# Row sums of squares in one accumulator, context operand made earlier, modulation rounds in pairs of steps ahead of the attention

## The chip, the cores and the metric

The kernel runs on one core of one Trainium2 chip. The metric is the device time in microseconds of one execution, by the median of several runs; less is better. In the profile PE is TensorE (PEld its weight loads), DVE is VectorE, ACT is ScalarE, POOL is GpSimd and SP is SyncE, which here only issues DMAs. PE reads its operands from SBUF and writes to PSUM, which has eight banks; the matmuls here run in fp32 or in a form of it (fp32r).

## What is computed

Two transformer blocks in a row on x, 512 positions by 1024 channels. What the change touches lies in the front of the first block:

```python
mod_l = jnp.split((jax.nn.silu(c) @ ada_w[l] + ada_b[l])[:, None, :], 6, axis=-1)
mod_c = jnp.split((jax.nn.silu(c_ctx) @ ada_w[l] + ada_b[l])[None, None, :], 6, axis=-1)

h = _modulate(_rmsnorm(x, norm1_g[l]), mod_l[0], mod_l[1])
hc = _modulate(_rmsnorm(xc, norm1_g[l]), mod_c[0], mod_c[1])
z = h @ w_in[l]
...
kvc = hc @ w_in[l][:, ATT_W:3 * ATT_W]
...
att = _neighbourhood_attention(q, k, v, kc, vc, na_rpb[l], rows)
y = _mix_out(att, z, ...)
x = x + mod_l[2] * y

h2 = _modulate(_rmsnorm(x, norm2_g[l]), mod_l[3], mod_l[4])
x = x + mod_l[5] * _conv_ffn(h2, ...)
```

`_rmsnorm` divides each row by the root of its mean square, and `_modulate(h, shift, scale)` is `h * (1 + scale) + shift`. Parts 0 and 1 of the modulation are needed at once, for h and hc; parts 2 to 5 only behind the attention. The second block (stick-breaking attention, a gated convolution, a feed-forward part) is not touched.

## The kernel before

Everything is kept transposed, channels on the 128 partitions, so that x is eight slices of 128 x 512 (`xs`) and the context eight of 128 x 256 (`cs`). A matmul in full precision is three matmuls (`mm3`, lines 164 to 166): each operand is split into a rounded high half and a rest (hi on ACT, lo on DVE).

The order on every engine is that of the code; each engine works through its own instructions in turn, and a wait holds all that stand behind it. SP issues its DMAs in program order too.

The front runs in these stages.

- **Row sums of squares of x.** For each slice as it lands, ACT or DVE (in turn) squares it, and PE adds it up over channels with four matmuls by a column of ones into `ssb` (line 485), 32 matmuls in all. `rsqrt_col` makes the reciprocal root of it (ACT's root, then DVE), `bcast` spreads that over the partitions by four matmuls, and ACT copies it into `rxs`.
- **First projection** (`first_*`). For each of eight slices k: 1 MB of modulation weights arrives (`first_ada`), `first_rows` multiplies it by the conditioning columns (16 records on PE), `first_mod` turns the result into shift and scale of slice k, `first_h` makes h[k], `first_split` splits 128 x 768 of the weights w_in, and `first_mm` adds 18 matmuls into six banks `first`.
- **u and q** (`p_u`, `p_q`): four weight pieces of 256 columns. Beside them the taps of a depthwise convolution of length 31 run on DVE (`tap_v`), some after every tile.
- **Context operand** (`make_hc`): for each slice k of the context, DVE multiplies, ACT adds the shift and rounds (hi), DVE makes the rest (lo). Two slices are made per call: slices 0 and 1 behind the first tile of the last query piece, 2 and 3 behind its second, 4 and 5 behind the first value tile, 6 and 7 behind the second.
- **v** (`v_tile`): four tiles from h, then two from hc (the first uses of hc), for each half of the columns; keys (`keys`, from h and hc) partly between the two halves, partly inside the attention.
- **Attention**: a loop over 32 blocks n. In one pass PE makes the scores of block n (`s`), turns the weights of block n-3 (`pt`) and applies those of n-6 (`o`); DVE adds the bias and finds the minimum (`e`, line 889), ACT takes the exponent, DVE its reciprocal (`rd`), POOL scales. `e` of block n stands on DVE behind `rd` of block n-1, which waits for ACT's exponent of n-1.
- **Rest of the modulation** (`ada_*`). Parts 2 to 5 are two rounds of eight steps. `ada_fetch` issues the four DMAs of a step (1 MB), `ada_step` runs its four matmuls (128 x 512, eight records) into a bank, `ada_end` finishes a round. `ada_tick` ends a round if one is due, fetches one step, and runs one step if more than two are fetched. It is called behind most tiles of u, q and v, and in the attention from block 7 on (AD0) at every second block. So seven steps run ahead of the first context value tile, the eighth behind the second one, the first round ends in the second half of v, and the second round's eight steps and its end lie in the attention.

Tiles lie in a pool of 80 slots of 128 x 512, reused when their readers are done; weight pieces in three buffers `wraw`, so that a DMA into one waits until DVE has split what was there.

Of the kernel before, what the change touches and what calls it, by code (L numbers as in the profile page):

```python
# [9 lines left out]
F32 = mybir.dt.float32  # L10
# [111 lines left out]
AD0 = 7  # L122
# [13 lines left out]
def program(ctx: ExitStack, tc: tile.TileContext, A, outT):  # L136
# [14 lines left out]
    def bank(name="bank", cols=T):  # L151
        return ps.tile([P, cols], F32, tag="b", name=name, padded_shape=[P, T])
# [324 lines left out]
    ssb = bank("sums", cols=4)  # L477
    for k in range(KD):
        t = slot(name="sq")
        if k % 2:  # L480
            V.tensor_mul(t, xs[k], xs[k])
        else:
            S.activation(t, xs[k], AF.Square)
        for i in range(4):
            PE.matmul(ssb[:, i : i + 1], t[:, i * P : (i + 1) * P], ones, start=k == 0 and i == 0,
                      stop=k == KD - 1, skip_group_check=True)
# [8 lines left out]
    def first_w(p):  # L495
        wr = wraw_p.tile([P, 2048], F32, tag="wraw", name="wraw")[:, : 2 * NF * P].rearrange("p (k n) -> p k n", k=2)
        nc.sync.dma_start(wr, w_in[p * 256 : (p + 1) * 256, W0 : W0 + NF * P].rearrange("(k p) n -> p k n", p=P))
        for kk in range(2):
            fw[2 * p + kk] = wr[:, kk, :]
# [44 lines left out]

    first_ada(0)
    first_w(0)
    first_ada(1)
    first_ada(2)
    first_w(1)
    first_rows(0)  # L550
    rx = rsqrt_col(ssb, 4)
    first_split(0)
    first_mod(0)
    rxb = bcast(rx, 4)
    rxs = slot(name="rxs")
    S.activation(rxs, rxb, AF.Copy)
    first_h(0)
    first_rows(1)
    first_split(1)
    first_mod(1)  # L560
    first_h(1)
    first += [bank(f"first{m}") for m in range(NF)]
    for k in range(KD):
        if k + 3 < KD:
            first_ada(k + 3)
        if k in (1, 3):
            first_w(2 + k // 2)
        if k == 5:
            ws.load(0)
        if k + 2 < KD:  # L570
            first_rows(k + 2)
            first_split(k + 2)
        first_mm(k, range(3))
        if k + 2 < KD:
            first_mod(k + 2)
            first_h(k + 2)
        first_mm(k, range(3, NF))
        del fw[k]
    ws.need(0)
# [59 lines left out]

    ROUNDS = (4, 5, 8, 9), (6, 7, 10, 11)  # L640
    ada_live, ada_todo, ada_bank = [], [(r, kk) for r in range(2) for kk in range(KD)], {}

    def ada_fetch():
        if ada_todo:
            r, kk = ada_todo.pop(0)
            raw = [slot(name="ada") for _ in range(4)]
            for t, c in zip(raw, ROUNDS[r]):
                nc.sync.dma_start(t, A["ada_w"][kk * P : (kk + 1) * P, c * T : (c + 1) * T])
            ada_live.append((r, kk, raw))

    def ada_step():
        r, kk, raw = ada_live.pop(0)
        if kk == 0:
            ada_bank[r] = bank("adab")
        for g in range(4):
            ada_matmul(ada_bank[r], g, kk, raw[g], kk == 0, kk == KD - 1)
        if kk == KD - 1:
            t = slot(name="arow")
            S.activation(t, ada_bank[r], AF.Copy)
            ada_ends.append((r, t))  # L660

    def ada_end():
        r, t = ada_ends.pop(0)
        b = ada_bank.pop(r)
        for q in range(4):
            PE.matmul(b[:, 4 * q : 4 * q + 4], t[:, q * P : (q + 1) * P], pick, start=True, stop=True)
        for g in (0, 2):
            j = 4 * ROUNDS[r][g]
            V.tensor_add(mod[:, j : j + 8].rearrange("p (g q) -> p g q", q=4),
                         b[:, :16].rearrange("p (q g) -> p g q", g=4)[:, g : g + 2],  # L670
                         pc("ada_b", j, 8).rearrange("p (g q) -> p g q", q=4))

    ada_ends = []

    def ada_tick(ahead=2):
        if ada_ends:
            ada_end()
        ada_fetch()
        if len(ada_live) > ahead or not ada_todo and ada_live:
            ada_step()  # L680

# [13 lines left out]
    ada_fetch()  # L695
    run(tiles(p_u, (0,), h, evac_u))
    ada_fetch()
# [32 lines left out]
    ada_tick()  # L730
    rcbs = slot(name="rcbs", cols=CTX)
    S.activation(rcbs, bcast(rc[0], 2), AF.Copy)
    hc = [None] * KD
# [19 lines left out]
    for i in range(4):  # L753
        V.tensor_scalar(vt_[i], vt_[i], mv[:, 2 * i : 2 * i + 1], sd[:, i : i + 1], op0=ALU.subtract, op1=ALU.mult)
        G.tensor_mul(vt_[i], vt_[i], rows[0][:, 0:256])
        G.tensor_add(vt_[i], vt_[i], rows[0][:, 256:512])
        t = slot(F32R, "vn")
        vn.append((t[:, :256], t[:, 256:]))
    for m in range(2):
        run(tiles(p_q[1], (m,), h, lambda m, b: evac_q(2 + m, b)))  # L760
        make_hc(2 * m, 2 * m + 1)
        ada_tick()
# [68 lines left out]
    for i in range(4):  # L831
        v_tile(p_v[0], 0, h, i, vt[i])
        if i < 2:
            make_hc(4 + 2 * i, 5 + 2 * i)
        split(*vn[i], vt_[i])
        if i % 2:
            ada_tick()
    for i in range(2):
        v_tile(p_v[0], 0, hc, i, vc[i])
    ada_step()  # L840
# [167 lines left out]
    for n in range(NA + OUT + 1):  # L1008
# [45 lines left out]
        if n >= AD0 and (n - AD0) % 2 == 0 and (ada_todo or ada_live or ada_ends):  # L1054
            ada_tick()
# [528 lines left out]
```

## Time and profile before

| | us |
|---|---|
| median of three runs | 1434.5 (1433.75 to 1435.11) |
| the profiled execution | 1432.46 |
| its span, first to last instruction | 1430.7 |
| mean granted clock of PE | 0.988 of full |

A row of the profile groups equal instructions or shows single ones: L485 is line 485 of the kernel, `out<-in` names the tiles, and what stands in brackets is how long the engine had sat idle and what ended that. Records of PE are pipelined and overlap, so a step of work is read from the start of one matmul to the start of the next. One fp32 matmul that isn't fp32r shows as two records.

### The profile page before, as it was taken

The numbers are of one execution on the slowest core, as the hardware profiler recorded it, in microseconds if no ns is written. First come the engines' busy times: TensorE is split into PE (matmuls) and PEld (weight loads), VectorE is DVE, ScalarE is ACT, GpSimd is POOL, SyncE is SP. The second block draws the span as 40 slices with busy tenths as digits, with TensorE's granted clock in tenths as the row PEclk, the third lists the DMA queues.
The fourth block names the chain that finished last, engine by engine and source line by source line (L and its number), as shares of the span: only waits on it lengthen the run. The fifth ranks groups of instructions, "written<-read, shape, count | busy, mean of one in ns | idle before, by whom it ended". The sixth has DMA issues, their size and how long they took to land.

```text
span 1430.7 us, 18856 instructions
## 1 busy us (share of the span) xinstructions
PE 1397.2 (98%) x7594; PEld 1175.1 (82%) x7594; DVE 776.9 (54%) x1138; ACT 555.5 (39%) x888; POOL 223.2 (16%) x210
## 2 busy tenths in 40 slices
PE   8997999999999999999999999999999999999996
PEld 6776986889888888888988888888888888888886
DVE  3578675746444344344448874445266866664224
ACT  3342255635433333233345543223454444443221
POOL 0021213110201111022010112000161111110102
PEclk9998999999999999999999999999999999999998
DMA  9574257332223222323164113222311322322221
GB/s 355 173 261 148 78 155 243 97 122 89 89 88 118 87 90 70 111 93 102 54 194 131 60 60 112 94 89 90 117 58 61 118 88 91 115 82 81 82 80 59
DMA packets 141878, 160.42 MB, mean 112 GB/s; under 512 B 5600, under 2 KB 119520, under 8 KB 141792
## 3 DMA queue, kind: packets, MB, share of 16 engines
q1 hardware_dynamic: 140352, 156.91, 33.8%
q10 hardware_dynamic: 1440, 2.31, 0.5%
q8 instruction: 59, 0.97, 0.3%
q14 instruction: 27, 0.22, 0.0%
HBM read 147.67 MB, written 2.10 MB: 105 GB/s over the span
## 4 chain that ended last, share of the span: by engine, by line
PE 75%; DVE 4%; ACT 1%; POOL 1%; issue 1%; DVEq 0%; POOLq 0%; ACTq 0%
PE bank L165 23%; PE bank L164 23%; PE bank L166 23%; PE z L1366 1%; PE sums L383 1%; POOL acc L1503 1%; DVE wlo L210 1%; PE v L164 1%; PE v L165 1%; PE v L166 1%; PE wT L1387 1%; PE bc L391 0%; DVE fo L1558 0%; DVE fo L1554 0%; PE o L164 0%
## 5 line engine op out<-in xcount | busy, mean ns | idle before, releaser
L210 DVE TENSOR_TENSOR wlo<-wraw,whi 128x1024 fp32r<-128x1024 f32 (+1 forms) x214 | 278.4, 1308 | 140.0 <-ACT whi L202 139.9
L165 PE MATMUL bank<-h_lo,whi 128*128 128x512 f32 (+1 forms) x816 | 306.2, 375 | 0.1
L166 PE MATMUL bank<-h_hi,wlo 128*128 128x512 f32 (+1 forms) x816 | 304.9, 374 | 0.8 <-DVE wlo L210 0.8
L164 PE MATMUL bank<-h_hi,whi 128*128 128x512 f32 (+1 forms) x816 | 305.7, 375 | 0.0
L202 ACT ACTIVATE whi<-wraw 128x1024 fp32r<-128x1024 f32 (+1 forms) x214 | 220.6, 1035 | 121.4 <-PE bank L165 107.3
L164 PEld LDWEIGHTS bank<-h_hi,whi 128*128 128x128 f32 x816 | 154.1, 189 | 28.6 <-ACT u L684 0.8
L166 PEld LDWEIGHTS bank<-h_hi,wlo 128*128 128x128 f32 x816 | 154.0, 189 | 28.7 <-DVE wlo L210 1.6
L165 PEld LDWEIGHTS bank<-h_lo,whi 128*128 128x128 f32 x816 | 154.1, 189 | 28.2 <-DVE h_lo L1494 0.3
L164 PE MATMUL bank<-act_hi,whi 128*128 128x512 f32 (+1 forms) x374 | 141.1, 377 | 0.8 <-ACT sq L1477 0.8
L165 PE MATMUL bank<-act_lo,whi 128*128 128x512 f32 (+1 forms) x374 | 140.8, 376 | 0.0
L166 PE MATMUL bank<-act_hi,wlo 128*128 128x512 f32 (+1 forms) x374 | 140.8, 376 | 0.0
L172 POOL TENSOR_TENSOR act_lo<-cv,act_hi 128x512 fp32r<-128x512 f32 x44 | 61.2, 1392 | 422.2 <-ACT act_hi L171 384.2
L164 PE MATMUL bank<-hb_hi,whi 128*128 128x512 f32 x288 | 115.8, 402 | 0.0
L166 PE MATMUL bank<-hb_hi,wlo 128*128 128x512 f32 x288 | 112.6, 391 | 0.0
L165 PE MATMUL bank<-hb_lo,whi 128*128 128x512 f32 x288 | 112.4, 390 | 0.0
L164 PEld LDWEIGHTS bank<-act_hi,whi 128*128 128x128 f32 x374 | 70.4, 188 | 14.0 <-ACT sq L1477 1.0
L166 PEld LDWEIGHTS bank<-act_hi,wlo 128*128 128x128 f32 x374 | 70.4, 188 | 13.0
L165 PEld LDWEIGHTS bank<-act_lo,whi 128*128 128x128 f32 x374 | 70.4, 188 | 12.8
L171 ACT ACTIVATE act_hi<-cv 128x512 fp32r<-128x512 f32 x44 | 27.8, 633 | 129.3 <-DVE cv L1208 72.9
L166 PEld LDWEIGHTS bank<-hb_hi,wlo 128*128 128x128 f32 x288 | 54.1, 188 | 11.5
L164 PEld LDWEIGHTS bank<-hb_hi,whi 128*128 128x128 f32 x288 | 54.2, 188 | 9.4
L165 PEld LDWEIGHTS bank<-hb_lo,whi 128*128 128x128 f32 x288 | 54.3, 188 | 9.1
(359 smaller groups left out, 2375.9 us busy)
## 6 DMA issues: line engine op xcount, KB each, us to landing
wraw<-in_w_in SPq DMA_DIRECT2D x23, 1024.0 KB, 5.1
wraw<-in_ffn_w_up SPq DMA_DIRECT2D x22, 1024.0 KB, 4.9
wraw<-in_w_up SPq DMA_DIRECT2D x22, 1024.0 KB, 4.9
ada<-in_ada_w SPq DMA_DIRECT2D x64, 256.0 KB, 5.7
ada<-in_ada_first SPq DMA_DIRECT2D x32, 256.0 KB, 6.5
wraw<-in_w_out SPq DMA_DIRECT2D x8, 1024.0 KB, 5.2
wraw<-in_ffn_w_down SPq DMA_DIRECT2D x8, 1024.0 KB, 5.0
wraw<-in_w_down SPq DMA_DIRECT2D x8, 1024.0 KB, 5.0
```

The costliest lines, as they stand in the source:

```text
L164: PE.matmul(out, lhs[0], rhs[0], start=start, stop=False, **kw)
L165: PE.matmul(out, lhs[0], rhs[1], start=False, stop=False, **kw)
L166: PE.matmul(out, lhs[1], rhs[0], start=False, stop=stop, **kw)
L171: S.activation(hi, src, AF.Copy)
L172: (eng or V).tensor_sub(lo, src, hi)
L202: S.activation(h, src, AF.Copy)
L210: V.tensor_sub(l, src, h)
L383: PE.matmul(b[:, i : i + 1], a[:, blk * P : (blk + 1) * P], ones, start=(j == 0), stop=(j == len(parts) - 1))
L1366: PE.matmul(z, qs2[hp][a][j][:, b * P : (b + 1) * P], ks2[hp][j][:, :nk], start=a == 0, stop=a == 1)
L1387: PE.transpose(pt[:, c * P : (c + 1) * P], w_[:, c * P : (c + 1) * P], ident)
L1503: G.tensor_add(acc3[:, ts], acc3[:, ts], t)
```

## The change

Four things change.

1. **Sums of squares.** ACT squares all eight slices; DVE adds the squares of slices 0 to 6 into one accumulator `xacc`; PE sums over channels once, by eight matmuls (`col_sums` of the accumulator and the last square). The root is taken ahead of the first `first_rows`, the copy `arow` stands behind it on ACT.
2. **First weights.** `first_w` loads 384 KB for one slice instead of 768 KB for two, each behind the modulation weights of its slice.
3. **Context operand.** `make_hc(0, 1)` stands ahead of the last query piece, and each later pair one tile earlier; 6 and 7 are made behind the first value tile.
4. **Modulation.** `ada_tick` runs two steps (and a fetch behind each) if so many are fetched; five steps are fetched inside the first projection (k from 3 to 7); there is a tick behind the first tile of u, and none in the attention. All sixteen steps run ahead of the first context value tile, in eight ticks of two. The first round ends behind the first tile of the last query piece, the second in the second half of v.

```diff
-    ssb = bank("sums", cols=4)
+    xacc = slot(name="xacc")
     for k in range(KD):
-        t = slot(name="sq")
-        if k % 2:
-            V.tensor_mul(t, xs[k], xs[k])
-        else:
-            S.activation(t, xs[k], AF.Square)
-        for i in range(4):
-            PE.matmul(ssb[:, i : i + 1], t[:, i * P : (i + 1) * P], ones, start=k == 0 and i == 0,
-                      stop=k == KD - 1, skip_group_check=True)
+        xsq = xacc if k == 0 else slot(name="sq")
+        S.activation(xsq, xs[k], AF.Square)
+        if 0 < k < KD - 1:
+            V.tensor_add(xacc, xacc, xsq)
     sqrt_table()
...
     def first_w(p):
-        wr = wraw_p.tile([P, 2048], F32, tag="wraw", name="wraw")[:, : 2 * NF * P].rearrange("p (k n) -> p k n", k=2)
-        nc.sync.dma_start(wr, w_in[p * 256 : (p + 1) * 256, W0 : W0 + NF * P].rearrange("(k p) n -> p k n", p=P))
-        for kk in range(2):
-            fw[2 * p + kk] = wr[:, kk, :]
+        if p % 2 == 0:
+            wr_[0] = wraw_p.tile([P, 2048], F32, tag="wraw", name="wraw")
+        fw[p] = wr_[0][:, p % 2 * 1024 : p % 2 * 1024 + NF * P]
+        nc.sync.dma_start(fw[p], w_in[p * P : (p + 1) * P, W0 : W0 + NF * P])
...
-    def ada_tick(ahead=2):
+    def ada_tick(n=2):
         if ada_ends:
             ada_end()
-        ada_fetch()
-        if len(ada_live) > ahead or not ada_todo and ada_live:
+        for _ in range(min(n, len(ada_live))):
             ada_step()
+            ada_fetch()
...
-    first_ada(0)
-    first_w(0)
-    first_ada(1)
-    first_ada(2)
-    first_w(1)
-    first_rows(0)
-    rx = rsqrt_col(ssb, 4)
+    for k in range(3):
+        first_ada(k)
+        first_w(k)
+    rx = rsqrt_col(col_sums((xacc, xsq), range(4)), 4)
     first_split(0)
-    first_mod(0)
+    first_rows(0)
     rxb = bcast(rx, 4)
+    first_mod(0)
...
     for k in range(KD):
         if k + 3 < KD:
             first_ada(k + 3)
-        if k in (1, 3):
-            first_w(2 + k // 2)
-        if k == 5:
+            first_w(k + 3)
+        elif k == 5:
             ws.load(0)
+        if k >= 3:
+            ada_fetch()
...
-    ada_fetch()
     run(tiles(p_u, (0,), h, evac_u))
-    ada_fetch()
+    ada_tick()
...
+    make_hc(0, 1)
     for m in range(2):
         run(tiles(p_q[1], (m,), h, lambda m, b: evac_q(2 + m, b)))
-        make_hc(2 * m, 2 * m + 1)
+        make_hc(2 + 2 * m, 3 + 2 * m)
         ada_tick()
...
         v_tile(p_v[0], 0, h, i, vt[i])
-        if i < 2:
-            make_hc(4 + 2 * i, 5 + 2 * i)
+        if i == 0:
+            make_hc(6, 7)
...
-    ada_step()
     kg = keys()
...
-        if n >= AD0 and (n - AD0) % 2 == 0 and (ada_todo or ada_live or ada_ends):
-            ada_tick()
```

The built programs show where this puts the instructions. PE at its start, before (`sums` are the row sums, `ada` the rows of `first_rows` and the columns of `first_mod`, `bc` the spread root, `first` the first projection):

```order
L485 MATMUL sums<-ones,sq 128x1 x32
L473 MATMUL ada<-ada,sc 32x256 x8
L518 MATMUL ada<-sel,arow 128x2 x2
L391 MATMUL bc<-ident,ro 128x128 x4
L473 MATMUL ada<-ada,sc 32x256 x8
L518 MATMUL ada<-sel,arow 128x2 x2
L473 MATMUL ada<-ada,sc 32x256 x8
```

PE at its start, changed, from the last of the eight sums on:

```order
L382 MATMUL sums<-ones,xacc 128x1
L382 MATMUL sums<-ones,sq 128x1
L472 MATMUL ada<-ada,sc 32x256 x8
L390 MATMUL bc<-ident,ro 128x128 x4
L515 MATMUL ada<-sel,arow 128x2 x2
L472 MATMUL ada<-ada,sc 32x256 x8
L515 MATMUL ada<-sel,arow 128x2 x2
L472 MATMUL ada<-ada,sc 32x256 x8
```

The 32 sums became eight, and `bc` moved ahead of the first `sel` matmuls; behind that the groups up to the first projection are the same.

DVE ahead of the last query piece, before (`vgt` is the normed gate, `q_lo` a query's low half, `cacc` the convolution's taps, `cs` and `hc` the context slice and its low half):

```order
L749 TENSOR_SCALAR sd<-mv 128x4
L751 RECIPROCAL sd<-sd 128x4
L754 TENSOR_SCALAR vgt<-vgt,mv,sd 128x256 x4
L175 SCALAR_TENSOR_TENSOR q_lo<-bank,q_hi 128x512
L210 TENSOR_TENSOR wlo<-wraw,whi 128x1024
L630 SCALAR_TENSOR_TENSOR cacc<-ag,par,cacc 128x510
L630 SCALAR_TENSOR_TENSOR cacc<-ag,par,cacc 128x509
L630 SCALAR_TENSOR_TENSOR cacc<-ag,par,cacc 128x508
L630 SCALAR_TENSOR_TENSOR cacc<-ag,par,cacc 128x507
L740 SCALAR_TENSOR_TENSOR cs<-cs,gs,rcbs 128x256
L742 SCALAR_TENSOR_TENSOR hc<-cs,mod_113,hc 128x256
```

DVE at that place, changed:

```order
L747 TENSOR_SCALAR sd<-mv 128x4
L749 RECIPROCAL sd<-sd 128x4
L752 TENSOR_SCALAR vgt<-vgt,mv,sd 128x256 x4
L738 SCALAR_TENSOR_TENSOR cs<-cs,gs,rcbs 128x256
L740 SCALAR_TENSOR_TENSOR hc<-cs,mod_113,hc 128x256
L738 SCALAR_TENSOR_TENSOR cs<-cs,gs,rcbs 128x256
L740 SCALAR_TENSOR_TENSOR hc<-cs,mod_113,hc 128x256
L174 SCALAR_TENSOR_TENSOR q_lo<-bank,q_hi 128x512
L209 TENSOR_TENSOR wlo<-wraw,whi 128x1024
L672 SCALAR_TENSOR_TENSOR cacc<-ag,par,cacc 128x510
```

The pair of slices 0 and 1 now stands ahead of `q_lo` and the taps; three further pairs follow at the places where the three others of before stood, each one pair further on, and the place behind the second value tile is empty.

SP in the first projection, before (`in_ada_first` is the first projection's modulation, `in_ada_w` the later rounds', `in_w_in` weights, `in_ctxT` the context):

```order
L504 DMA ada<-in_ada_first 128x512 x8
L497 DMA wraw<-in_w_in 128x2x768
L504 DMA ada<-in_ada_first 128x512 x8
L497 DMA wraw<-in_w_in 128x2x768
L504 DMA ada<-in_ada_first 128x512 x4
L189 DMA wraw<-in_w_in 128x8x256 x4
L583 DMA cs<-in_ctxT 128x2x256 x4
L648 DMA ada<-in_ada_w 128x512 x8
```

SP there, changed:

```order
L501 DMA ada<-in_ada_first 128x512 x4
L494 DMA wraw<-in_w_in 128x768
L551 DMA ada<-in_ada_w 128x512 x4
L501 DMA ada<-in_ada_first 128x512 x4
L494 DMA wraw<-in_w_in 128x768
L551 DMA ada<-in_ada_w 128x512 x4
L188 DMA wraw<-in_w_in 128x8x256
L551 DMA ada<-in_ada_w 128x512 x12
L188 DMA wraw<-in_w_in 128x8x256 x3
L625 DMA cs<-in_ctxT 128x2x256 x4
L551 DMA ada<-in_ada_w 128x512 x8
L188 DMA wraw<-in_w_in 128x8x256
```

Five later steps (20 DMAs of 256 KB) are now issued inside the first projection, ahead of the second to fourth weight pieces and of the context. In the attention, seven groups of four such DMAs are gone from among the bias and key moves on SP, and on PE eight groups of four `adab` matmuls and the round's end, each of which stood between `o` of one block and `s` of the next.

## Rows read from the trace of the kernel before

**Rows 1.** The page: span; busy us, share and instructions of each engine.
```profile
span 1430.7 us, 18856 instructions
...
PE 1397.2 (98%) x7594; PEld 1175.1 (82%) x7594; DVE 776.9 (54%) x1138; ACT 555.5 (39%) x888; POOL 223.2 (16%) x210
```

**Rows 2.** Windows: stretch, length, busy PE PEld DVE ACT POOL, PE clock, DMA share, GB/s.
```profile
18.40:27.87 9.47, 8.17 (x66) 4.80 (x65) 4.31 (x11) 3.53 (x7) 0.00 (x0) 1.00 1.04 397
...
124.54:142.24 17.70, 10.40 (x56) 9.01 (x56) 14.21 (x29) 6.06 (x15) 0.00 (x0) 0.71 0.18 60
132.00:140.00 8.00, 5.20 (x21) 4.56 (x21) 6.81 (x16) 2.89 (x9) 0.00 (x0) 0.50 0.01 2
209.89:257.76 47.87, 44.90 (x410) 33.43 (x411) 27.90 (x83) 26.94 (x60) 16.49 (x22) 0.93 0.66 199
```

**Rows 3.** Chain of waits, PE: waiter, what it waited for, us, times, longest.
```profile
PE v L164 <- ACT hc L741: 7.3, 4, 3.9
...
PE adab L473 <- DMA ada<-in_ada_w: 3.0, 2, 1.9
```

**Rows 4.** Timeline, first 30 us: start, us, engine, line, operation, [idle before].
```profile
4.68 13.79 PE L485 MATMUL sums<-ones,sq 128*128 128x1 f32 x64 [4.68 <-ACT sq L483]
...
9.09 0.69 DVE L481 TENSOR_TENSOR sq<-xs 128x512 f32<-128x512 f32 x1 [0.56 <-DMA xs<-in_xTc]
...
18.40 1.93 PE L473 MATMUL ada<-ada,sc 128*32 128x256 f32 x16
...
21.54 0.16 DVE L330 SCALAR_TENSOR_TENSOR ro<-rt,rr 128x4 f32<-128x4 f32 x1
...
26.87 1.07 PE L473 MATMUL ada<-ada,sc 128*32 128x256 f32 x16
...
27.87 0.50 PE L164 MATMUL first<-h_hi,whi 128*128 128x512 f32 x1
```

**Rows 5.** Timeline, PE around the first context value tile.
```profile
122.97 0.28 PE L166 MATMUL v<-whi,h_lo 128*128 128x256 f32 x1
...
123.33 0.28 PE L166 MATMUL v<-whi,h_lo 128*128 128x256 f32 x1
...
123.54 1.06 PE L473 MATMUL adab<-ada,sc 128*32 128x512 f32 x8
...
124.54 0.38 PE L164 MATMUL v<-whi,hc 128*128 128x256 f32 x1
```

**Rows 6.** Timeline, PE: one end of a round.
```profile
150.47 0.95 PE L666 MATMUL adab<-ident,arow 128*128 128x4 f32 x8
```

**Rows 7.** Timeline, DVE: a query's low half, later two pairs of context slices.
```profile
88.34 0.69 DVE L175 SCALAR_TENSOR_TENSOR q_lo<-bank,q_hi 128x512 fp32r<-128x512 f32 x1 [3.16 <-ACT q_hi L174]
...
122.73 0.48 DVE L740 SCALAR_TENSOR_TENSOR cs<-cs,gs,rcbs 128x256 f32<-128x256 f32 x1
...
125.25 0.48 DVE L742 SCALAR_TENSOR_TENSOR hc<-cs,mod,hc 128x256 fp32r<-128x256 f32 x1 [0.58 <-ACT hc L741]
...
131.60 0.48 DVE L742 SCALAR_TENSOR_TENSOR hc<-cs,mod,hc 128x256 fp32r<-128x256 f32 x1 [0.57 <-ACT hc L741]
```

**Rows 8.** Chain of waits, DVE, 170 to 290 us.
```profile
DVE e L889 <- PE s L881: 9.6, 6, 6.7
```

**Rows 9.** Timeline, DVE in the attention at two blocks in a row.
```profile
216.90 0.69 DVE L889 CUSTOM_DVE_ANT_0 e<-s,bias 128x512 f32<-128x512 f32 x1
...
218.77 0.69 DVE L889 CUSTOM_DVE_ANT_0 e<-s,bias 128x512 f32<-128x512 f32 x1
```

**Rows 10.** Timeline, PE in the attention after the second of these blocks.
```profile
219.83 2.71 PE L473 MATMUL adab<-ada,sc 128*32 128x512 f32 x4 [1.94 <-DMA ada<-in_ada_w]
```

**Rows 11.** Windows, ahead of the attention.
```profile
40.00:60.00 20.00, 20.00 (x129) 14.67 (x128) 9.48 (x17) 6.48 (x11) 0.00 (x0) 1.00 0.25 87
60.00:120.00 60.00, 60.00 (x325) 46.23 (x324) 44.14 (x64) 24.75 (x41) 17.20 (x19) 1.00 0.76 263
```

**Rows 12.** DMA issues: queue, count, KB each, median us to landing.
```profile
ada<-in_ada_w SPq DMA_DIRECT2D x64, 256.0 KB, 5.7
```

More of the change, by code (lines that the diff above doesn't have):

```diff
@@ L495, in first_w @@
     def first_w(p):
-        wr = wraw_p.tile([P, 2048], F32, tag="wraw", name="wraw")[:, : 2 * NF * P].rearrange("p (k n) -> p k n", k=2)
-        nc.sync.dma_start(wr, w_in[p * 256 : (p + 1) * 256, W0 : W0 + NF * P].rearrange("(k p) n -> p k n", p=P))
-        for kk in range(2):
-            fw[2 * p + kk] = wr[:, kk, :]
+        if p % 2 == 0:
+            wr_[0] = wraw_p.tile([P, 2048], F32, tag="wraw", name="wraw")
+        fw[p] = wr_[0][:, p % 2 * 1024 : p % 2 * 1024 + NF * P]
+        nc.sync.dma_start(fw[p], w_in[p * P : (p + 1) * P, W0 : W0 + NF * P])
+    wr_ = [None]
     def first_ada(k):
@@ L543, in first_mm, with ada_fetch, ada_step, ada_end @@
             mm3(first[m], (hi[:, m * P : (m + 1) * P], lo[:, m * P : (m + 1) * P]), h[k], k == 0, k == KD - 1)
-    first_ada(0)
-    first_w(0)
-    first_ada(1)
-    first_ada(2)
-    first_w(1)
+    ROUNDS = (4, 5, 8, 9), (6, 7, 10, 11)
+    ada_live, ada_todo, ada_bank = [], [(r, kk) for r in range(2) for kk in range(KD)], {}
+    def ada_fetch():
+        if ada_todo:
+            r, kk = ada_todo.pop(0)
+            raw = [slot(name="ada") for _ in range(4)]
+            for t, c in zip(raw, ROUNDS[r]):
+                nc.sync.dma_start(t, A["ada_w"][kk * P : (kk + 1) * P, c * T : (c + 1) * T])
+            ada_live.append((r, kk, raw))
+    def ada_step():
+        r, kk, raw = ada_live.pop(0)
+        if kk == 0:
+            ada_bank[r] = bank("adab")
+        for g in range(4):
+            ada_matmul(ada_bank[r], g, kk, raw[g], kk == 0, kk == KD - 1)
+        if kk == KD - 1:
+            t = slot(name="arow")
+            S.activation(t, ada_bank[r], AF.Copy)
+            ada_ends.append((r, t))
+    def ada_end():
+        r, t = ada_ends.pop(0)
+        b = ada_bank.pop(r)
+        for q in range(4):
+            PE.matmul(b[:, 4 * q : 4 * q + 4], t[:, q * P : (q + 1) * P], pick, start=True, stop=True)
+        for g in (0, 2):
+            j = 4 * ROUNDS[r][g]
+            V.tensor_add(mod[:, j : j + 8].rearrange("p (g q) -> p g q", q=4),
+                         b[:, :16].rearrange("p (q g) -> p g q", g=4)[:, g : g + 2],
+                         pc("ada_b", j, 8).rearrange("p (g q) -> p g q", q=4))
+    ada_ends = []
+    def ada_tick(n=2):
+        if ada_ends:
+            ada_end()
+        for _ in range(min(n, len(ada_live))):
+            ada_step()
+            ada_fetch()
[3 more added lines that the diff above has]
+    rx = rsqrt_col(col_sums((xacc, xsq), range(4)), 4)
+    first_split(0)
     first_rows(0)
-    rx = rsqrt_col(ssb, 4)
-    first_split(0)
+    rxb = bcast(rx, 4)
     first_mod(0)
-    rxb = bcast(rx, 4)
     rxs = slot(name="rxs")
     S.activation(rxs, rxb, AF.Copy)
+    del rxb
     first_h(0)
     first_rows(1)
-    first_split(1)
     first_mod(1)
     first_h(1)
+    first_split(1)
     first += [bank(f"first{m}") for m in range(NF)]
@@ L578, in program @@
         del fw[k]
+    wr_.clear()
     ws.need(0)
@@ L637, in conv_taps @@
             conv.append(acc)
[L640 to L673, printed above, removed]
-    def ada_tick(ahead=2):
-        if ada_ends:
-            ada_end()
-        ada_fetch()
-        if len(ada_live) > ahead or not ada_todo and ada_live:
-            ada_step()
     def evac_u(m, b):
@@ L729, in program @@
     run(tiles(p_q[0], (1,), h, lambda m, b: evac_q(m, b)))
-    ada_tick()
     rcbs = slot(name="rcbs", cols=CTX)
     S.activation(rcbs, bcast(rc[0], 2), AF.Copy)
+    ada_tick()
     hc = [None] * KD
```

3 lines of the change are left out of this document (removed).

## The prediction

> **What bounds the kernel now.** I read the page first. PE is busy for 1397.2 of 1430.7 us [rows 1]; no other engine comes near. So the kernel can get shorter in two ways: PE does less, or it loses less at the few places where it isn't full. The page can't show these; the windows view does. Four stretches matter here [rows 2]: 18.40 to 27.87, where PE already works on small groups but the first projection hasn't begun; 124.54 to 142.24, with 10.4 us busy in 17.7 us and a mean granted clock of 0.71; inside it 132 to 140, at 0.50, which is the lower of the two levels (1.2 instead of 2.4 GHz); and the attention's middle from 209.89 to 257.76, at 0.93.
>
> The chain of waits says who held PE: the value tiles waited 7.3 us for `hc`, once 3.9 us in one piece, and the later modulation steps 3.0 us for their DMA [rows 3]. The low clock of 132 to 140 follows directly behind the first. The timeline of the start [rows 4] shows what no wait names: 64 records of sums keep PE from 4.68 to 18.47 us, although the last slice of x was there at 9.09.
>
> **Part 1, the sums.** ACT needs for the last square about what DVE's took, 0.69 us, and DVE's add the same again: with the slice at 9.09 and the add of the seventh beside it, the accumulator and the last square are there by about 10.0. Then 16 records at 13.79/64 = 0.215 us make 3.4, so the sums end at 13.4 instead of 18.47. Behind them stand the same groups as before up to the first matmul of the projection, 9.47 us from 18.40 to 27.87 [rows 2, 4]. I keep that length: the root comes earlier relative to them (`ro` was ready only 3.2 us behind the sums, since ACT's root stood behind the copy of `first_rows`), but the copy, h and its splits still follow one another. The first projection then begins at 22.9, **5.0 us sooner**. Bounds: no gain at all if the modulation weights land no sooner than now needed; at most about 7, if the earlier root also takes 2 us out of the chain. DMA moves 397 GB/s there [rows 2]. The last slice of x had landed at 9.09, so the first 1.05 MB of modulation is there 2.6 us later, at about 11.8, and each further slice (1.05 and 0.39 MB) 3.6 us behind the one before: slice 2 at 19.0, needed about 1.4 us ahead of 22.9. That is room, but not for 2 us more in every case. Hence 5.0 and not 7.
>
> Rate: the 16-record group at 18.40 took 1.93 us, the one at 26.87 only 1.07, though the window shows 1.00 granted for both [rows 2, 4]. So PE, at work without a break since 4.68, was still at its lower level at 18.40 and had reached the upper one by 26.87. The groups between the two stand ahead of the projection afterwards too, so I take the rise to come with them again, ahead of the first matmul. The Trainium skill (TensorE: Matmul & The Clock Gate, Part 1) says that the throttled state is the default and that activity releases it; the two durations agree. That rule speaks against taking 24 of 32 matmuls out of the start: by it the rise could come later against the work, and the sum would be that of the first rival.
>
> The loads of 384 KB for one slice bring four DMAs more on SP, but the first pair's second half no longer stands ahead of slice 1's modulation. I cost that at nothing: SP is held up by the bytes here, not by its issues.
>
> **Part 2, the modulation ahead of the attention.** A step costs PE 1.0 us: `adab` starts at 123.54, the next matmul at 124.54 [rows 5]; the end of a round at most 0.95 [rows 6], I take 0.9. Eight steps and one end move ahead of the attention: 8 x 1.0 + 0.9 = **8.9 us more** there. Bounds: 8.0, as two steps in a row share one hand-over, and, if a tick finds its weights not landed, each such wait on top. The supply: from 40 to 60 us DMA moves 87 GB/s, from 60 to 120 it moves 263 [rows 11]. Five steps more in the first are 5.2 MB, so 350 GB/s; in the second eleven steps instead of nine, 2.1 MB more, so 298. Both lie under the 397 seen at the start. A step is fetched at least two ticks ahead of its use; a tile of u or q between two ticks is 24 matmuls of twice 0.12 us [rows 5], 5.8, and two steps, so over 15 us, against 5.7 to landing [rows 12]. One early step stands ahead of the last slice's weights on SP; these land at 11.8 + 7 x 3.6 + 2.6, about 40 us, and are needed behind five slices of at least 18 x 0.24 = 4.3 us, not before 44. I take no wait.
>
> **Part 3, the context operand.** Undisturbed, the two context tiles are 48 matmuls of 0.12 us (122.97 to 123.33 are three of them [rows 5]), with the hand-over 6.0; they took 17.7 [rows 2]. How much of the 11.7 us comes back depends on DVE, which is late: it waited last at `q_lo`, 88.34 [rows 7], then works almost without idle through taps and pairs. That query tile moves by -5.0 + 3 steps (four steps ahead of it instead of one) = -2.0 us. A pair costs 3.0 us (122.73 to 125.73), and the third ended at 132.1 [rows 7]. At that place of the program four pairs are now done, and two small adds of the round's end: 132.1 - 2.0 + 3.0 + 0.2 = 133.3. PE comes to the first context tile at 124.54 - 5.0 + 9 steps + one end = 129.4 and needs the last slice 7/8 of 2.9 us later, at 131.9; its high half is ready about 0.5 ahead of 133.3. So about 1.2 us of waiting stay, no low clock: 7.2 instead of 17.7, **10.5 us less**. Bounds: 11.7 if DVE keeps up; if DVE is 5 us later than I reckon, 5.5. What is late next: DVE's backlog no longer drains during PE's stall, so the values' low halves and the gating's sums come some 5 us behind PE instead of being caught up; the banks that PE takes next were written two to three tiles ahead, which just covers it.
>
> **Part 4, the attention.** Without the steps PE has 8 x 1.0 + 0.9 us less to do and no DMA to wait for (the step at 219.83 had waited 1.94 and then took 2.71 for four records [rows 10]). If PE alone set the pace, that and the longest stall (6.7) would come back, 15.6 us. But `e` of one block follows `e` of the block ahead by 1.87 us [rows 9], a loop over DVE, ACT and DVE that doesn't hold PE in it. In all the attention `e` waited for PE's scores 9.6 us, in six waits, the longest 6.7 [rows 8]; only these can shrink. I take **9.6 us less**; bounds 6.7 (the dry stretch alone) and 15.6.
>
> **The sum**: -5.0 + 8.9 - 10.5 - 9.6 = -16.2. Against the profiled execution's own time, 1432.46 (1.8 us lie around its span), that is 1416.3; the runs' median lies 2.0 above that execution, so 1418.3 by the median. I say **1418**. What a measurement of this kernel can tell from no change is about 0.2%, 2.9 us.
>
> **Rivals.**
> - *The array stays at its lower rate into the projection.* For: the start has 48 records of 0.215 us less of PE work. If the first slice of the projection runs at the lower level, its 18 matmuls take 8.6 instead of 4.3 us, and the gain of part 1 shrinks to 0.7: 1422.5. Against: the groups that stood between the two durations are all kept.
> - *DVE comes later than reckoned.* For: it has no idle time to give between 88 and 132. With it 5 us later part 3 gives 5.5 instead of 10.5, and if the clock falls again some 2 more is lost: 1423 to 1425.
> - *The attention follows PE.* Against: `e` every 1.87 us. It would give 15.6: 1412.
> - *Slower: the pairs run the weights dry.* A tick that catches its step not landed held PE like the one in the attention, whose wait on `e` was 6.7 us. From the third such tick on (20 us against 16.2) the kernel is slower, about 1423 + 6.7 for each further one, say 1438 to 1445 with three to four and the low clock behind them. Against: 298 and 350 of 397 GB/s, and the fetch 15 us ahead.
> - *The change doesn't do what it says*: DVE's order leaves the last pair as late, and the start follows DMA: parts 1 and 3 nil, 8.9 - 9.6 remain: 1433.8, no change.
>
> **How the numbers follow.** The forecast (1414 to 1421 with its bounds) 0.60; low rate at the start 0.10; DVE later 0.12; attention follows PE 0.09; dry weights 0.05, of it 0.04 slower; no change 0.02; the rest, a place that I haven't seen, on both sides 0.02. The likeliest gives 1418. The range 1411 to 1425 leaves the dry case and no change out, and takes in the others. Faster 0.93, same 0.03, slower 0.04.
>
> **What would show it.** Sums ending at 13 to 14 us and the first `first` matmul at 22 to 24; a wait of `v` for `hc` under 2 us and granted clock 1.00 through both context tiles; sixteen steps in eight groups of some 2.0 us ahead of the first context tile, without a DMA wait; the attention's middle shorter by 9 to 10 us with `e` bound to 1.87 us and PE waiting there instead. It is wrong if the 16-record groups stay at 1.9 us into the projection, if `adab` shows waits for `in_ada_w`, or if PE waits for `sgo`, `v_lo` or `wlo` between the context tiles and the attention.

## The result and the profile after

The changed kernel takes 1421.9 us (four runs, 1419.04 to 1423.39) where the kernel before took 1434.12 beside it (four runs, 1433.56 to 1435.11). That is 12.2 us less by the medians; by the ratio, 0.9912 (95% interval 0.9894 to 0.9929), it is 12.6, or 0.9%. The forecast was 1418 with a range of 1411 to 1425: direction and range hold, but four of the 16.2 us forecast did not come. The profiled execution (1421.66 us) is 10.8 shorter than that of before.

The page of the kernel after, as [rows 1]: TensorE's busy time fell by 14.4 us, the span by only 10.8, so it now stands idle longer than before.

```profile
span 1419.9 us, 18781 instructions
...
PE 1382.8 (97%) x7546; PEld 1166.0 (82%) x7546; DVE 778.9 (55%) x1140; ACT 557.8 (39%) x892; POOL 221.1 (16%) x210
```

The timeline of PE at the start of the kernel after, as [rows 4]:

```profile
10.93 0.56 PE L382 MATMUL sums<-ones,xacc 128*128 128x1 f32 x2 [10.93 <-DVE xacc L481]
...
13.91 0.56 PE L382 MATMUL sums<-ones,sq 128*128 128x1 f32 x2
14.40 1.93 PE L472 MATMUL ada<-ada,sc 128*32 128x256 f32 x16
16.27 2.08 PE L390 MATMUL bc<-ident,ro 128*128 128x128 f32 x8
...
22.32 1.93 PE L472 MATMUL ada<-ada,sc 128*32 128x256 f32 x16
24.19 0.80 PE L163 MATMUL first<-h_hi,whi 128*128 128x512 f32 x1
```

The sums are short now, but begin 0.9 us later than reckoned, and the last 16-record group ahead of the projection still takes 1.93 us, where before it took 1.07 [rows 4]. The projection's first five matmuls start 0.4 to 0.6 us apart, later ones 0.23: there the rate rose. The projection began 3.7 us sooner and ended 2.9 sooner.

Chain of waits of PE, kernel after, the lines that answer to [rows 3]:

```profile
PE pt L910 <- POOL e L903: 6.0, 4, 2.4
...
PE v L163 <- ACT hc L739: 2.1, 2, 1.6
```

The wait for the later modulation's DMA is gone, that for the context operand has shrunk from 7.3 to 2.1 us, and one in the attention, for the tile that GpSimd (POOL) scales, has grown from 0.5 to 6.0 us. A pair of steps, as [rows 5], and two blocks of the attention in a row, as [rows 9], in the timelines of PE and DVE of the kernel after:

```profile
128.76 1.92 PE L472 MATMUL adab<-ada,sc 128*32 128x512 f32 x16
...
214.37 0.69 DVE L887 CUSTOM_DVE_ANT_0 e<-s,bias 128x512 f32<-128x512 f32 x1
...
216.25 0.69 DVE L887 CUSTOM_DVE_ANT_0 e<-s,bias 128x512 f32<-128x512 f32 x1
```

A step costs 0.96 us, and `e` follows `e` by 1.88, before by 1.87. Windows of the kernel after around the two context tiles (their first matmul starts at 130.62, the first one behind them at 140.75):

```profile
132.00:134.00 2.00, 1.02 (x9) 0.82 (x7) 1.96 (x4) 0.00 (x0) 0.00 (x0) 1.00 0.52 122
134.00:136.00 2.00, 0.88 (x3) 0.48 (x3) 0.89 (x3) 1.01 (x3) 0.00 (x0) 0.90 1.08 378
136.00:138.00 2.00, 1.94 (x8) 1.93 (x9) 1.93 (x5) 2.00 (x9) 0.00 (x0) 0.50 0.07 25
138.00:140.00 2.00, 2.00 (x15) 2.00 (x14) 2.00 (x5) 0.80 (x3) 0.00 (x0) 0.74 0.00 0
```

The two waits of PE in them:

```profile
134.60 0.39 PE L163 MATMUL v<-whi,hc 128*128 128x256 f32 x1 [1.58 <-ACT hc L739]
...
136.06 0.58 PE L163 MATMUL v<-whi,hc 128*128 128x256 f32 x1 [0.55 <-ACT hc L739]
```

The granted clock falls to its lower level between 134 and 136 and is still there from 136 to 138. The timeline of DVE of the kernel after shows why the last pair came late:

```profile
107.50 0.95 DVE L738 SCALAR_TENSOR_TENSOR cs<-cs,gs,rcbs 128x256 f32<-128x256 f32 x1
...
111.54 1.06 DVE L740 SCALAR_TENSOR_TENSOR hc<-cs,mod,hc 128x256 fp32r<-128x256 f32 x1 [0.64 <-ACT hc L739]
...
131.77 0.42 DVE L171 TENSOR_TENSOR v_lo<-v,v_hi 128x256 fp32r<-128x256 f32 x1
132.10 1.51 DVE L672 SCALAR_TENSOR_TENSOR cacc<-ag,par,cacc 128x501 f32<-128x501 f32 x2
133.53 0.48 DVE L738 SCALAR_TENSOR_TENSOR cs<-cs,gs,rcbs 128x256 f32<-128x256 f32 x1
...
136.04 0.49 DVE L740 SCALAR_TENSOR_TENSOR hc<-cs,mod,hc 128x256 fp32r<-128x256 f32 x1 [0.58 <-ACT hc L739]
```

A low half and two taps stand ahead of the last pair, which PE needs from 132.9 on; it ends at 136.5, not at 133.3.

The account of the two profiled executions, by the start times of the same matmuls:

| | before | after | change so far |
|---|---|---|---|
| first matmul of u | 69.97 | 67.10 | -2.9 |
| first context tile | 124.54 | 130.62 | +6.1 |
| first matmul of the keys | 155.67 | 153.15 | -2.5 |
| first scores of the attention | 173.76 | 171.24 | -2.5 |
| end of the last `o` | 281.95 | 270.38 | -11.6 |
| span | 1430.7 | 1419.9 | -10.8 |

### The profile page after: what moved, and what is told of

Same layout as the page of the kernel before. It is cut to its first block, busy times and chain, and to the rows that moved or that the text cites. A ratio compares the mean times of both kernels' runs of the same rounds, so it can differ in the third digit from the quotient of the medians.

```text
span 1419.9 us, 18781 instructions
## 1 busy us (share of the span) xinstructions
PE 1382.8 (97%) x7546; PEld 1166.0 (82%) x7546; DVE 778.9 (55%) x1140; ACT 557.8 (39%) x892; POOL 221.1 (16%) x210
## 4 chain that ended last, share of the span: by engine, by line
PE 86%; DVE 7%; ACT 3%; issue 2%; DMA 1%; POOL 1%; SPq 0%; DVEq 0%; ACTq 0%; POOLq 0%
PE bank L164 24%; PE bank L163 24%; PE bank L165 24%; PE v L163 1%; PE v L165 1%; PE v L164 1%; PE sums L382 1%; PE first L163 1%; DVE wlo L209 1%; PE z L1362 1%; PE first L165 1%; PE first L164 1%; DVE e L887 1%; POOL acc L1499 1%; PE ada L472 1%
## 5 line engine op out<-in xcount | busy, mean ns | idle before, releaser
L165 PEld LDWEIGHTS bank<-hb_hi,wlo 128*128 128x128 f32 x288 | 54.0, 188 | 11.5
```

What stands on the lines that cost most here:

```text
L165: PE.matmul(out, lhs[1], rhs[0], start=False, stop=stop, **kw)
```

## The experiments

Every ratio is to the kernel before, run beside on the same chip. "Attention" is the time from the first scores to the end of the last `o`: 108.2 us before, 99.1 after.

**Part 1 alone**, on the kernel before: the sums, the weight loads and the start's order of the diff above, without the fetches in the projection.

```diff
+        xsq = xacc if k == 0 else slot(name="sq")
+        S.activation(xsq, xs[k], AF.Square)
+        if 0 < k < KD - 1:
+            V.tensor_add(xacc, xacc, xsq)
...
+    rx = rsqrt_col(col_sums((xacc, xsq), range(4)), 4)
```

> The kernel before with part 1 alone (the squares summed in one accumulator, the start's order and loads that go with it). By the prediction's term: first matmul of the first projection at 22.9 us instead of 27.87, 5.0 us less, 1429.1. By what the trace after shows (sums from 10.9 to 14.5, every small group at its lower rate until 128x512 matmuls run): first matmul at about 24.2, the projection's end 2.9 us sooner, 1431.2; since taps and context operand hang on the projection, this passes on whole. Rival: VectorE still brings the context operand late and eats the gain, 1433.5 to 1434.

Measured: 1429.95 us, ratio 0.9965 (0.9951 to 0.9979), which is 5.0 us (3.0 to 7.0) less. The timeline of PE at its start:

```profile
13.93 1.93 PE L473 MATMUL ada<-ada,sc 128*32 128x256 f32 x16
...
18.41 1.07 PE L473 MATMUL ada<-ada,sc 128*32 128x256 f32 x16
...
21.41 1.69 PE L473 MATMUL ada<-ada,sc 128*32 128x256 f32 x16
23.03 0.79 PE L164 MATMUL first<-h_hi,whi 128*128 128x512 f32 x1
```

Here the rate rose at the second group and fell again inside the third, behind a wait of 1.4 us; the projection ended 4.1 us sooner than before. The median bears out the term of 5.0, the trace neither it nor the 2.9 of the other trace: the gain depends on where in the start the rate rises. The rival that VectorE eats it is out. The context tiles waited 7.1 us as before: what the start gives, all behind it gets.

**Part 3 alone**, on the kernel before.

```diff
+    make_hc(0, 1)
     for m in range(2):
         run(tiles(p_q[1], (m,), h, lambda m, b: evac_q(2 + m, b)))
-        make_hc(2 * m, 2 * m + 1)
+        make_hc(2 + 2 * m, 3 + 2 * m)
...
-        if i < 2:
-            make_hc(4 + 2 * i, 5 + 2 * i)
+        if i == 0:
+            make_hc(6, 7)
```

> The kernel before with part 3 alone (context operand one tile earlier). By the prediction's term taken by itself: 10.5 us less, 1423.6; by the stretch that the trace after shows, 7.7 less, 1426.4. Theory that VectorE's queue sets it and that the eight modulation steps ahead of the context tiles are the cover: the fourth pair ends at about 135 (137.0 before), PE comes to the first context tile at 124.5 as before and waits about 8 us for it, then the lower clock again; the two tiles end 1.5 to 2.5 us sooner, 1431.6 to 1432.6.

Measured: 1433.14 us, ratio 0.9985 (0.9973 to 0.9997), 2.2 us less, a little above the range expected. Chain of waits of PE:

```profile
PE v L164 <- ACT hc L741: 4.9, 3, 4.0
...
PE v L165 <- DVE wlo L210: 1.3, 1, 1.3
```

From their first matmul to the next one behind them, the two tiles take 14.4 instead of 17.6 us. But PE comes to them 1.6 us later, counted from the projection's end: it first waits 1.3 us for a low half of weights (`wlo`), which the pair moved forward now holds up on DVE. That was not expected, and it leaves 1.7 us. Without the modulation steps ahead of the tiles the operand is still far behind. The term of 10.5 isn't part 3's own.

**Parts 2 and 4 alone**, on the kernel before (the ticks of the diff above, five fetches in the projection; sums and `make_hc` as before).

```diff
+        if k >= 3:
+            ada_fetch()
...
-    def ada_tick(ahead=2):
+    def ada_tick(n=2):
...
-        if n >= AD0 and (n - AD0) % 2 == 0 and (ada_todo or ada_live or ada_ends):
-            ada_tick()
```

> The kernel before with parts 2 and 4 alone (steps in pairs beside queries and values, none in the attention; sums and context operand as before). By the prediction's terms: 8.9 more ahead, 9.6 less in the attention, 1433.4, the same. Theory that the steps ahead of the context tiles also give VectorE the time that it lacks: PE comes there at 133.5, the fourth pair ends at about 140, the two tiles take about 11.3 instead of 17.7 us with operand places unchanged; attention and what follows 8.3 less: 1427 to 1428.

Measured: 1426.69 us, ratio 0.9944 (0.9932 to 0.9957), 8.0 us less. Chain of waits of PE:

```profile
PE v L163 <- ACT hc L742: 3.2, 2, 2.6
```

PE comes to the first context tile at 133.36 instead of 124.54, waits 3.2 instead of 7.3 us, and the two tiles take 12.0 instead of 17.6: 5.6 of the 8.8 us lie in time that PE had stood idle or at its lower clock. The keys begin 2.1 us later than before, the attention takes 99.3. So of the three the two modulation parts carry most; the three singles add to 15.2 us, the whole change measured 12.6 by its ratio, within the intervals.

**The last pair one place earlier**, on the kernel after.

```diff
-        make_hc(2 + 2 * m, 3 + 2 * m)
+        make_hc(*((2, 3), (4, 5, 6, 7))[m])
         ada_tick()
...
-        if i == 0:
-            make_hc(6, 7)
```

> The kernel after with the last pair of context slices (6 and 7) made at the place of the pair ahead of it, in front of the first value tile's low half and two taps. Theory (the wait of 2.1 us and the low clock behind it come from VectorE's queue order): pair done at about 133.1 instead of 136.4, waits for the operand under 0.3 us, granted clock 1.00 from 130 to 144, 3 to 4 us less than after: 1418 to 1419. Rival: the weights' and the values' low halves, now 3 us later on VectorE, are waited for instead: 0 to 1 us less, 1421 to 1422.

Measured: 1420.19 us, ratio 0.9895 (0.9881 to 0.9909). Chain of waits of PE:

```profile
PE mix L165 <- DVE vn L171: 2.6, 2, 2.2
```

Window from 130 to 144 us, as [rows 2]:

```profile
130.00:144.00 14.00, 11.42 (x92) 10.69 (x89) 12.24 (x24) 7.71 (x17) 0.00 (x0) 1.00 0.23 75
```

There is no wait for `hc` left, the granted clock is 1.00 throughout, and the two tiles and the next, 72 matmuls, take 8.7 us instead of 13.0 from the first start to that of the gating's products (`mix`). These then wait 2.6 us for the low half of `vn`, which stands on DVE behind what was pushed back, and the keys begin only 1.5 us sooner than in after. So the order theory is right, and the rival is right in its kind, with another tile than it named.

**Taps put off**, on last_pair_earlier.

```diff
+    lv.rate = 1.6
     for i in range(4):
         v_tile(p_v[0], 0, h, i, vt[i])
...
+    lv.rate = 4.5
     ws.limit = 1 << 30
```

> last_pair_earlier with the convolution's taps given out slower beside the value tiles (rate 1.6 instead of 3.3, some 6 taps of 0.75 us put off) and faster beside the keys (4.5). Theory (VectorE has too much to do beside the value tiles; the wait has only moved from the operand to the gating's vn, 2.6 us): that wait goes, 2.2 to 2.6 us less than last_pair_earlier, 1417.5 to 1418. Rival: the taps put off are waited for in the keys or in the attention instead: the same as last_pair_earlier, 1420 to 1421.

Measured: 1424.16 us, ratio 0.9927 (0.9915 to 0.9939). The wait for `vn` is gone, but the attention takes 106.3 us. Its timeline of DVE:

```profile
219.32 0.68 DVE L171 TENSOR_TENSOR cat_lo<-o,cat_hi 64x512 fp32r<-64x512 f32 x1 [1.46 <-ACT cat_hi L170]
220.03 5.00 DVE L672 SCALAR_TENSOR_TENSOR cacc<-ag,par,cacc 128x500 f32<-128x500 f32 x4
224.95 0.16 DVE L895 RECIPROCAL rd<-den 128x1 f32<-128x1 f32 x1
225.02 0.67 DVE L887 CUSTOM_DVE_ANT_0 e<-s,bias 128x512 f32<-128x512 f32 x1
```

The taps that are left must be done by a fixed block of the attention; four stand there in a row, 5.0 us, and `e` behind them. PE's longest wait for `e` grew to 5.2 us. VectorE's backlog was not cured, only moved to where it costs more: the rival holds.

**Taps brought forward**, on last_pair_earlier: 4.1 and 5.6 instead of 3.3 at the two tiles of u, 2.2 beside the values.

```diff
-    lv.rate = LR[0]
+    lv.rate = 4.1
     run(tiles(p_u, (0,), h, evac_u))
+    lv.rate = 5.6
...
     run(tiles(p_u, (1,), h, evac_u))
+    lv.rate = LR[0]
...
+    lv.rate = 2.2
     for i in range(4):
         v_tile(p_v[0], 0, h, i, vt[i])
```

> last_pair_earlier with four of the convolution's taps given out sooner, at the two u tiles where VectorE stands idle 1.1 and 6.2 us (rates 4.1 and 5.6), and as many fewer beside the value tiles (rate 2.2); from the keys on the taps stand as in last_pair_earlier. Theory (VectorE's work beside the values is conserved and shows where it is put: put off it was waited for in the attention, brought into idle time it is free): gating's wait for vn of 2.6 us under 0.5, attention 99 us long as in after, 1417.5 to 1418. Rival (the attention's loss in taps_later had another cause than the taps left over): gain as in taps_later only up to the keys and the attention long again, 1421 to 1424.

Measured: 1419.07 us, ratio 0.9902 (0.9888 to 0.9917). The wait for `vn` fell to 0.6 us and the keys began 2.3 us sooner than in last_pair_earlier, but the attention takes 102.1 us. The expectation was wrong on one point: the low rate lasted through both halves of the values, so 48 taps instead of 52 stood ahead of the attention's first block. Its timeline of DVE:

```profile
203.42 2.29 DVE L672 SCALAR_TENSOR_TENSOR cacc<-ag,par,cacc 128x499 f32<-128x499 f32 x3
205.62 0.15 DVE L897 RECIPROCAL rd<-den 128x1 f32<-128x1 f32 x1
205.81 0.69 DVE L889 CUSTOM_DVE_ANT_0 e<-s,bias 128x512 f32<-128x512 f32 x1
```

The last three taps stand in a row ahead of the tenth block's `e`.

**The start filled**, on the kernel after, ahead of the sums.

```diff
+    fill = bank("fill")
+    for k in range(6):
+        PE.matmul(fill, ident, xs[k], start=k == 0, stop=k == 6 - 1)
     rx = rsqrt_col(col_sums((xacc, xsq), range(4)), 4)
```

> The kernel after with six extra matmuls of 128x512 (fp32, ident on the first six slices of x as they land, into a bank of their own that nothing reads) in front of the sums. Theory (what the start lacks is TensorE's rate, since it stands idle to 10.9 us and then has only small groups): once the extra matmuls run at the upper level the 16 records of sums take about 2 instead of 3.5 us and each group of 16 modulation records 1.07 instead of 1.93; the first matmul of the projection comes at 20 to 22 us instead of 24.2 and is itself at the upper level, 3 to 5 us less than after: 1417 to 1419. Rival: the rate doesn't rise for them; at the lower level the six take 10 us or more and delay the sums, first matmul at 26 to 29, 1424 to 1427. Second rival: the chain over ScalarE and VectorE or the modulation's DMA sets the first matmul, 24 us, 1421.9.

Measured: 1417.28 us, ratio 0.9885 (0.9872 to 0.9898). Timeline of PE at its start:

```profile
3.64 8.43 PE L591 MATMUL fill<-xs,ident 128*128 128x512 f32 x12 [3.64 <-DMA xs<-in_xTc]
...
13.69 1.07 PE L472 MATMUL ada<-ada,sc 128*32 128x256 f32 x16
...
19.48 1.07 PE L472 MATMUL ada<-ada,sc 128*32 128x256 f32 x16
20.48 0.50 PE L163 MATMUL first<-h_hi,whi 128*128 128x512 f32 x1
```

All three groups take 1.07 us, the projection begins at 20.48 and ends 4.7 us sooner than in after, though the sums began 1.0 us later. It ends 2.1 us sooner even than in the earliest of the seven executions that have the start of after. Work that nothing reads makes the kernel faster: what the start lacked was rate, not work and not data. Neither rival holds.

**Dummy steps in the attention**, on the kernel after.

```diff
+    def dummy():
+        b = bank("dum")
+        for g in range(4):
+            ada_matmul(b, g, 0, dsrc, True, True)
...
+        if 7 <= n < 23 and n % 2:
+            dummy()
```

> The kernel after with eight dummy steps put back into the attention where the kernel before had them (the same four matmuls of 128x512 each, but on a resident tile, without DMA and without a round's end; their bank is read by nothing). The prediction's account (a loop over VectorE and ScalarE sets the pace, and only TensorE's dry stretch could be regained, bounds 6.7 and 9.6): the eight cost little, 0 to 3 us more than after, 1422 to 1425, the rest of the attention's gain being the missing DMA wait. Rival (the attention follows TensorE): they cost their 8 us, 1429 to 1430. In between, as after waits 3.9 us for GpSimd's scaled tile in these blocks and the first of the eight fall where keys fill TensorE: 4 to 5 us more, 1426 to 1427.

Measured: 1426.07 us (1421.32 to 1427.65), ratio 0.9932 (0.9916 to 0.9949). The runs lie too far apart for the total to tell 3 from 5 us; the attention's length in the trace tells: 102.4 instead of 99.1, 3.3 us for eight steps of 1.0, just above the 0 to 3 of the theory. PE's wait for `e` there falls from 6.0 to 2.8 us:

```profile
PE pt L910 <- POOL e L903: 2.8, 3, 1.1
```

The steps first fill time in which PE waits. Of the attention's gain of 9.1 us some 3.3 are the steps' work. The other 5.8 belong to what the dummies lack: the wait for the weights, their DMAs and the end of a round, which no run tells apart. One stall is most of it. In the timeline of DVE of the kernel before, behind the second row of [rows 9], comes

```profile
227.37 0.69 DVE L889 CUSTOM_DVE_ANT_0 e<-s,bias 128x512 f32<-128x512 f32 x1 [6.72 <-PE s L881]
```

This `e` came 8.60 us behind the one ahead of it; in after and with the dummies the same two stand 1.85 apart.

**GpSimd's two subtractions on VectorE**, on the kernel after, one run. What it undoes, in the timeline of POOL of the kernel after:

```profile
221.55 2.50 POOL L171 TENSOR_TENSOR cat_lo<-sgo,cat_hi 128x512 fp32r<-128x512 f32 x2 [2.56 <-ACT cat_hi L170]
224.02 1.36 POOL L903 TENSOR_SCALAR e<-e,rd 128x512 f32<-128x512 f32 x2
```

```diff
-            split(*cat[4 + i], sgo[i], eng=G)
+            split(*cat[4 + i], sgo[i])
```

> The kernel after with the low halves of the gating's two tiles subtracted on VectorE instead of GpSimd in the attention. Theory (TensorE's longest wait there, 2.4 us for GpSimd's scaled tile, comes from GpSimd's 2.5 us on those two subtractions): that wait falls to about 1.4 us, the other three stay, attention 1 us shorter, 98.1 instead of 99.1. Rival: VectorE, in the loop too, pays the 1.4 us itself and the attention stays 99 us or longer. One run's time can't tell 1 us; the attention's length in the trace is the reading.

Measured: 1419.15 us; the attention takes 100.0 us. The longest wait of PE for `e` fell from 2.4 to 1.6 us, but `e` of the sixteenth block came 4.74 instead of 3.53 us behind the one ahead of it, and the attention is 0.9 longer than in after: the rival holds, VectorE pays. The trace showed something else as well: in this execution the start's rate rose early (second group 1.72, third 1.07 us), and its projection ended 2.5 us sooner than that of after with the same instructions.

**Everything together**: taps_sooner with the filled start, then the same with the taps' rate back at 3.3 from the second half of the values on.

```diff
+    lv.rate = LR[0]
     kg = keys()
...
-    lv.rate = LR[0]
     ws.limit = 1 << 30
```

> taps_sooner with the six extra matmuls of start_filled ahead of the sums. If the start's rate and VectorE's order are two independent losses, they add: start_filled lay 4.6 below after, taps_sooner should lie 4 below it, 1413 to 1414. Rival: with everything on TensorE 3.7 us sooner VectorE or the DMA of the modulation is the later one again, a wait for hc, vn or in_ada_w comes back and half of one gain is lost, 1415 to 1417.

Measured: 1417.0 us, ratio 0.9887 (0.9869 to 0.9905), at the upper end of the rival's range, but not for the rival's reason. The waits ahead of the attention are the small ones of taps_sooner, but the attention takes 102.2 us: no gain over start_filled.

> all_together with the taps' rate back at 3.3 from the second half of the values on (it came back only behind the values, so that 48 instead of 52 taps stood ahead of the attention's first block and three in a row fell into its tenth). The taps then stand in the attention as in after. Theory (the 3 us that the attention lost in taps_sooner and all_together are these leftover taps): attention 99.1 instead of 102.2 us, gating's wait still under 0.7, 3 us less than all_together, 1413 to 1414.5. Rival (the attention is longer because all ahead of it is earlier, by a DMA or a weight's arrival): 102 us again and 1417.

Measured: 1414.26 us (1413.22 to 1416.05), ratio 0.9855 (0.9839 to 0.9872), 20.8 us less than before by it and 8 less than after. Chain of waits of PE:

```profile
PE pt L915 <- POOL e L908: 6.2, 4, 2.5
```

The attention takes 99.2 us, with 62 taps done at its seventh block as in after, and the gating waits 0.6. The three us were the leftover taps. The expectation held, although the projection ended 1.3 us later here than in all_together (63.6 against 62.3).

## Why the prediction was right, and where it was off

By its own steps, against the two traces. These add to 10.8 us, where the medians differ by 12.2: the traced execution of before lay 1.7 us below its median, that of after 0.2. So 1.4 of the 5.4 us that the traces fall short of the forecast lie in which executions were traced.

- **Part 1, forecast -5.0, in the trace -2.9.** The mechanism is right in its first half: shorter sums bring the projection forward. The size is off in the profiled execution. Sums ended at 14.5, not 13.4: ACT's squares and DVE's adds follow one another, and the accumulator was ready at 10.9, not 10.0. That is 1.1 of the 2.1 us. The rest is the step "I take the rise to come with them again, ahead of the first matmul": in that trace it came inside the projection, behind its first five matmuls. This was the first rival, given 0.10, in a milder form, for that took all 18 matmuls of the first slice at the lower rate. The traces of seven executions with this start (after, part 1 alone and five experiments that leave the start alone) show projections that end 2.9 to 5.4 us sooner than before, in five of them 2.9 to 3.6, with all three groups at 1.93 us; start_filled shows that the rate is the cause. By the medians part 1 alone gave its 5.0 (3.0 to 7.0), but with later sums and a rate that came at another place than forecast, so that this agreement is in part luck. The Trainium skill (TensorE: Matmul & The Clock Gate, Part 1) has the throttled state as the default that activity releases, and the durations in start_filled agree with it.
- **Part 2, forecast +8.9, in the trace +7.9.** PE came to the first context tile 8.95 us later against the start, with nine steps and a round's end ahead of it, and the step that stood behind the context tiles (1.1 with its hand-over) is gone: the lower bound. A pair of steps takes 1.92 us. No wait for their DMA, as forecast.
- **Part 3, forecast -10.5, in the trace -7.5.** The two tiles took 10.1 instead of the 7.2 us forecast. The wait itself was 2.1 us against 1.2, so nearly as forecast; "no low clock" was wrong. In last_pair_earlier, without wait and low clock, the tiles take 5.9 us; so some 2.1 of the 10.1 are the lower clock. The pair came 3.2 us later than reckoned, and PE 1.2. Of the 3.2, 2.1 are the start's missing gain, passed on to VectorE (`q_lo` at 88.49, not 86.3). The first pair, moved to where GpSimd norms the gate, took 5.1 us instead of the 3.0 that I took from later pairs; the four taps that had stood there (4.6 us) took 3.1 at their later place and set most of that off. The rival "DVE later" came true in part.
- **Part 4, forecast -9.6, in the trace -9.1**, and 0.8 given back behind the attention. `e` stands some 1.87 us apart at most blocks where nothing else is put on VectorE, and PE waits there, as forecast. The dummy steps show that the steps were neither free (the bound of 6.7 as the dry stretch alone) nor worth their full 8 us.
- **The sum as such.** Parts 2 and 3 were costed one by one, as if the one were a loss and the other a gain. The experiments show that they share one stall: the steps alone shorten it by 5.6 us, the operand alone by 3.2, both by 7.5. From the projection's end to the first matmul of the keys, the steps alone cost 2.3 us, the operand alone gives 1.7, and the whole change costs 0.3, where the sum had a gain of 1.6. For a choice between the parts its terms would have been a wrong guide: by them parts 2 and 4 alone give 0.7 us, and they gave 8.0.
- **Its signs.** Sixteen steps in pairs without a DMA wait, an attention shorter by 9.1 us and PE waiting in it came as named. The end of the sums (14.5), the first matmul of the projection (24.2) and the wait for `hc` (2.1) lay just outside. The granted clock in the context tiles failed, and of the signs of being wrong one was there: the 16-record groups stayed at 1.9 us up to the projection.
- **Slips in the working.** By [rows 4] the third group starts 1.0 us ahead of the projection, not 1.4; and in the rival of the dry weights it is 1418.3 and 6.7 for each tick that gives the 1438 to 1445, not 1423 and more. Neither moves the forecast.

Left open: the 0.8 us behind the attention, where VectorE waits 3.0 us for a slice of x to be read back, against 1.7 before. No run was made on it.

## What to carry to other kernels

Work moved in front of a stall costs only what outlasts the stall (here 8.9 us of it shortened the stall by 5.6), so price such a move and the cure for the stall as one. An engine that is late everywhere gives its lateness from wait to wait: here the operand, the gating's tile and the attention's taps took turns until four taps went into time in which VectorE stood idle. Where a program begins with small groups and waits, try some matmuls that nothing reads before taking out more work: in the three executions with them the projection ended at 62.3 to 63.6 us, in the seven without at 64.6 to 67.1.

## What was not expected of the hardware

The window's granted clock is 1.00 up to the first change that it records: it reads 1.00 from 12 to 24 us of the kernel after, while its 16-record groups take 1.93 us; the durations of equal groups are the safer reading. When the rate rises varies from one execution to the next with the same instructions, which moves the projection's end by up to 2.5 us (64.6 or 67.1). The start of before does the same: in context_alone, which has it unchanged, all three groups took 1.93 us and the projection ended at 73.0, not 69.97. In all_together_taps_kept it rose within the extra matmuls and was lower once more behind a wait of 1.25 us at 18.4, the third group taking 2.23; in start_filled a wait of 1.40 us at the same place left the third group at 1.07. In after the lower clock came with a wait of 1.6 us and another of 0.6 in the context tiles; behind one of 2.2 us in the gating of last_pair_earlier it did not come. What it costs varies too: with the same matmuls and the same waits of 2.1 to 2.2 us, the two context tiles took 9.1 (low_half_on_vector), 10.1 (after), 10.6 (start_filled) and 11.5 us (idle_steps_in_attention). So the length of a wait alone doesn't tell, in these runs, whether the clock falls or what that costs.
